# Attention values by feature: values as the loaded operand in two halves of the array, probabilities divided before their transposes

## The chip, the cores and the metric

The kernel runs on one core of a Trainium2 chip. The metric is the device time of one execution in microseconds (us). TensorE (PE in the rows) multiplies, VectorE (DVE), ScalarE (ACT) and GpSimd (POOL) work element by element, and 16 DMA engines bring the weights. Each engine takes its instructions in the order of the built program.

## What is computed

Two layers of a decoder trunk on one sequence of 256 tokens with 1024 features, in float32. A layer has a mixer (8 causal attention heads of 64 features beside 4 groups of pooling channels, joined by one output projection) and a gated MLP with a short convolution. With one block of 256 keys, the attention is plain causal attention:

```
q, k, v, pz = split(h @ w_in)                       # 4 x 512 columns
p  = softmax(mask(q @ k.T * 64**-0.5))              # per head, 256 x 256, causal
ao = p @ v                                          # per head, 256 x 64
merged = concat(rms_norm(ao, attn_out_gain),        # over 512 features
                rms_norm(pool(pz), pool_out_gain))
x = x + gt1 * rms_norm(merged @ w_out, g_post_mix)
```

The heads are taken in pairs; a pair fills a chunk of 128 features, and there are four chunks, 0 to 3, in each layer.

## The kernel before

Weights stream in 1 MB pieces through four buffers on the SP queue (class `Stream`). Each piece is split into a high and a low float32r part by a cast on ACT (`hi`, L104) and a subtraction on DVE (`lo`, L105), and each large product is three TensorE instructions (`mm3`, L130 to L132). DVE also computes adaLN's dot products (L255), which come in among the mixer's steps.

The mixer's steps stand in the strings `ORDER` (L32), one per layer, in order of priority; from them and from its own estimates the tile framework writes each engine's instruction list. The steps around the change:

- `sc` (L545, L554): scores of a chunk, one bank of PSUM a head. DVE adds the mask and takes the row maximum (L560) and scales it (L563); ACT takes the exponential and its row sums (L567). Tokens are on partitions; per head there is a 128x128 piece (first 128 queries) and a 128x256 piece.
- `pt` (L570): three 128x128 transposes a head on TensorE (L576), copied by ACT to `pts` (L578): keys are then on partitions.
- `at` (L580): `pts` is the loaded operand, 128 columns, and 64 columns of `v` stream (L588). Six products a chunk, 12 instructions, since each float32 product is two passes. Tokens are on partitions in `ao`. DVE takes the reciprocal of the row sums (L592) and multiplies it in (L594, to `an`); ACT squares `an` and sums it by row, one instruction for each block of 128 tokens (L599, counted under `mean_sq`, L335).
- `tr` (L601): two transposes of `an` (L604) put features on partitions, and `merge` (L607) makes high and low parts with the gain, ACT (L609) and then DVE (L610).
- `as` (L672): DVE adds the four chunks' sums of squares (L675, L676), POOL takes the powers and a product (L677 to L680): 1 / rms of the attention group, and the ratio to the pool's.
- `gt` (L306): the gate: transposes `gT` (L299), two adds on DVE (L303, L304), a product (L313), then the transposes `gps` (L319). `ps` (L683): DVE scales the identity by POOL's ratio (`dg`, L687), and eight products with it (L693) bring the pool group to features. `wo` (L708) is the output projection `y` by chunk, 12 products each; the tail's last four chunks need `ps`.

Of the kernel before, what the change touches and what calls it, by code (L numbers as in the profile page):

```python
# [19 lines left out]
RAW_BUFS = 4      # weights as they come, 1 MB each  # L20
PART_BUFS = 8     # high and low parts, 128 x 1024 each
LEAD = 6          # parts made ahead of the tensor engine
ACT_BUFS = 13
DEFER = 6         # last chunks of the down projection, done one token block after the other
LAG = 2           # the down projection's distance behind the up projection
W4_BUFS = 7

# The mixer's steps in order of priority, per layer. kq: queries and keys to features; sc: scores and
# softmax; pt: probabilities transposed; at: values weighted; tr: attention to features; as: its sums;
# ph: pool projection; pc: its copy; sr: pool scale as a row; wi: windows; wp: pool products; ps: pool to  # L30
# features; gp, gt: gate; s2: scale of the next norm; wo: output projection; ah: parts of weights ahead.
ORDER = [  # L32
# [4 lines left out]
]  # L37

# columns of the per-feature vectors, per layer
# [5 lines left out]
class Stream:  # L45
    """Weights in the order of use: loads run RAW_BUFS ahead, parts LEAD ahead."""
# [7 lines left out]
    def load(self, dst, src):  # L54
        """A load to a place of its own, in its turn."""
        self.add(src, dst)
        self.done[-1] = True
# [35 lines left out]
    def ahead(self, n=LEAD):  # L93
        """High and low parts of the next weights: w = hi + lo exactly, both float32r."""
# [24 lines left out]
def trunk(ctx: ExitStack, tc: tile.TileContext, x, c, ct, vec, ident_d, tab_d, w_a1, w_gt, w_s2, w_g2,  # L119
# [125 lines left out]
    def table(func):  # L245
        """Brings the activation's table in ahead of its use."""
        tc.keep_in_program_order(nc.scalar.activation(dummy, dummy, func))

# [1 line left out]
    def dots(l, i, chs):  # L250
        """mod = silu(c) . w_ada + b_ada for two chunks of 128 columns."""
        t = st.raw(i)
        for n, ch in enumerate(chs):
            w = t[:, n * D:(n + 1) * D]
            nc.vector.tensor_tensor_reduce(  # L255
                w, w, cbc, 1.0, vecs[:, l, V_BADA + ch:V_BADA + ch + 1], op0=OP.mult, op1=OP.add,
                accum_out=mod[l][:, ch:ch + 1])
        st.free(i)
# [17 lines left out]
    def ada_gt(l, f, u, tag):  # L276
        """One round of a group of 1024 columns on the tensor engine: four column groups, rows alike."""
# [16 lines left out]
    def group_cols(l, f, s0, tag):  # L294
        """The group's columns to features on partitions, with their bias."""
# [10 lines left out]
    def gate_tile(l, f, tag):  # L306
        """gt * g_post as a row, on every partition."""
# [16 lines left out]
    def pre_coef(l, f, j0, j1):  # L324
        """A = (1 + sc) * g_pre for feature chunks j0..j1."""
# [11 lines left out]
    def rstd(ms, name):  # L337
        """(sum of the two mean squares + eps) ** -0.5."""
# [21 lines left out]
    def tail(mms, ys, g, ra, after):  # L360
        """Last products of each half of each block of tokens, and the block's way through the norms."""
# [30 lines left out]
    class Normed:  # L392
        """Chunks of the modulated norm as high and low parts, made from xn as asked for."""
# [13 lines left out]
        def make(self, j, src, on_act, b=None, between=None):  # L407
            """The chunk for both blocks of tokens, or for one."""
# [21 lines left out]
    def mixer(l, xn, gap):  # L430
# [5 lines left out]
        def w_in(o, k, b, w, c0, n=1):  # L436
            """Columns c0.. of the chunk's weights for one block of tokens, 512 to a bank."""
# [7 lines left out]
        if l == 0:  # L445
            # all columns at once, while the first weights come in
# [57 lines left out]
        # rotary on queries and keys while tokens are on partitions, then features  # L504
# [18 lines left out]
        def qk_trans(i, c2):  # L523
            """Chunks 2 c2, 2 c2 + 1 of the queries (i = 0) or the keys."""
# [15 lines left out]
        # causal attention, two heads to a chunk of 128 features  # L540
        rows = ((0, slice(0, 128)), (1, slice(128, 384)))
        sm, stt, pts, scp, outs, merged = {}, {}, {}, {}, {}, {}
        ssq = small(8, "ssq", 1).rearrange("p (b c) -> p b c", b=2)
# [10 lines left out]
        def soft_a(ch):  # L554
            sm[ch] = wk.tile([128, 2, 384], F32, tag="sm", name="sm", bufs=2)
            s_ = stt[ch] = small(16, "st")
            for hd in range(2):
# [7 lines left out]
                for b, sl in rows:  # L565
                    i = hd * 2 + b
                    nc.scalar.activation(sm[ch][:, hd, sl], sm[ch][:, hd, sl], AF.Exp, scale=0.125,  # L567
                                         bias=s_[:, 4 + i:5 + i], accum_out=s_[:, 8 + i:9 + i])

# [10 lines left out]
        def attend(ch):  # L580
            """Values weighted, then over the rows' sums; two heads side by side, tokens on partitions."""
            ao = bank("ps", "ao")
            for b in range(2):
                for hd in range(2):
                    o = ao[:, b * 128 + hd * 64:b * 128 + hd * 64 + 64]
                    for i in range(b + 1):
                        c0 = i * 512 + (2 * ch + hd) * 64
                        nc.tensor.matmul(o, pts[ch][:, hd, (b + i) * 128:(b + i + 1) * 128],  # L588
                                         vt[:, c0:c0 + 64], start=(i == 0), stop=(i == b),
                                         skip_group_check=True)  # L590
            s_ = stt[ch]
            nc.vector.reciprocal(s_[:, 12:16], s_[:, 8:12])  # L592
            an = outs[ch] = wk.tile([128, 256], F32, tag="an", name="an", bufs=2)
            nc.vector.tensor_mul(  # L594
                an.rearrange("p (b h d) -> p b h d", b=2, h=2),
                ao[:, 0:256].rearrange("p (b h d) -> p b h d", b=2, h=2),
                s_[:, 12:16].rearrange("p (h b) -> p b h", b=2)[:, :, :, None].to_broadcast([128, 2, 2, 64]))
            for b in range(2):
                mean_sq(an[:, b * 128:(b + 1) * 128], ssq[:, b, ch:ch + 1], 1.0 / 16.0)  # L599

        def attn_trans(ch):  # L601
            p = bank("ps", "aT")
            for b in range(2):
                nc.tensor.transpose(p[:, b * 128:(b + 1) * 128], outs[ch][:, b * 128:(b + 1) * 128], ident)  # L604
            merge(ch, p[:, 0:256], vecs[:, l, V_AGAIN + ch:V_AGAIN + ch + 1])
# [7 lines left out]
        # pooling channels  # L613
# [17 lines left out]
        def windows():  # L631
            """Windowed means less the token itself, as products with banded matrices over tokens."""
# [15 lines left out]
        def scale_row():  # L648
            """The pool's scale as a row, on every partition."""
# [344 lines left out]
```

## Time and profile before

| | |
|---|---|
| median of 3 runs | 611.97 us (611.96 to 611.98) |
| profiled execution: first to last instruction | 609.5 us |
| own time of the profiled execution | not listed apart; the runs' median is 2.5 us above the span |
| PE busy | 591.2 us, 97% |
| DVE busy | 482.1 us, 79% |
| ACT busy | 365.3 us, 60% |
| POOL busy | 23.8 us, 4% |
| weights and input read | 147.41 MB, 244 GB/s over the span |

The span is the execution's time from its first to its last instruction; around it lie a start and an end that no row shows. Attention takes some 40 us of each layer: from 59 to 101 us in layer 0 and from 354 to 394 us in layer 1. In both layers the output projection's products run on to the end of the mixer, at about 116 and 408 us. The rest is the combined input projection and the MLP, which the change does not touch.

### The profile page before, as it was taken

The numbers are of one execution on the slowest core, as the hardware profiler recorded it, in microseconds if no ns is written. First come the engines' busy times: TensorE is split into PE (matmuls) and PEld (weight loads), VectorE is DVE, ScalarE is ACT, GpSimd is POOL, SyncE is SP. The second block draws the span as 40 slices with busy tenths as digits, with TensorE's granted clock in tenths as the row PEclk, the third lists the DMA queues.
The fourth block names the chain that finished last, engine by engine and source line by source line (L and its number), as shares of the span: only waits on it lengthen the run. The fifth ranks groups of instructions, "written<-read, shape, count | busy, mean of one in ns | idle before, by whom it ended". The sixth has DMA issues, their size and how long they took to land.

```text
span 609.5 us, 9880 instructions
## 1 busy us (share of the span) xinstructions
PE 591.2 (97%) x3836; PEld 516.4 (85%) x3836; DVE 482.1 (79%) x847; ACT 365.3 (60%) x657; POOL 23.8 (4%) x64
## 2 busy tenths in 40 slices
PE   5999899999999999999999999999999999999995
PEld 3887578699999999999858878868999999999984
DVE  5998588679999998978558699555999887777753
ACT  4456787496466565566347578638755655656641
POOL 1000011200000000000010000110000000000001
PEclk9999999999999999999999999999999999999998
DMA  8999787867988877765419857526677766455001
GB/s 304 401 396 358 305 282 272 303 260 279 338 304 312 304 298 294 261 232 183 139 64 363 340 174 275 184 82 274 268 276 276 276 219 253 166 192 206 2 1 69
DMA packets 22769, 149.10 MB, mean 245 GB/s; under 512 B 2881, under 2 KB 3265, under 8 KB 6210
## 3 DMA queue, kind: packets, MB, share of 16 engines
q1 hardware_dynamic: 22722, 148.47, 65.7%
q8 instruction: 30, 0.49, 0.3%
q14 instruction: 17, 0.14, 0.1%
HBM read 147.41 MB, written 1.05 MB: 244 GB/s over the span
## 4 chain that ended last, share of the span: by engine, by line
PE 89%; DVE 5%; DMA 2%; ACT 2%; POOL 1%; issue 1%; POOLq 0%; SPq 0%; DVEq 0%; ACTq 0%
PE u L796 41%; PE d L130 7%; PE d L132 7%; PE d L131 7%; PE qk L131 2%; PE qk L130 2%; PE qk L132 2%; PE y L130 2%; PE y L132 2%; PE y L131 2%; DVE lo L105 1%; DMA raw<-w_up_d 1%; PE pz L130 1%; PE v L130 1%; PE pz L132 1%; PE pz L131 1%
## 5 line engine op out<-in xcount | busy, mean ns | idle before, releaser
L105 DVE TENSOR_TENSOR lo<-raw,hi 128x1024 fp32r<-128x1024 f32 (+1 forms) x184 | 217.7, 1196 | 27.4 <-ACT hi L104 27.2
L104 ACT CAST hi<-raw 128x1024 fp32r<-128x1024 f32 (+1 forms) x184 | 186.0, 1034 | 66.5 <-PE u L796 19.0
L796 PE MATMUL u<-hh,hi 128*128 128x256 f32 x704 | 182.0, 282 | 0.5 <-ACT hh L417 0.5
L796 PE MATMUL u<-hh,lo 128*128 128x256 f32 x704 | 181.8, 281 | 0.0
L796 PE MATMUL u<-hl,hi 128*128 128x256 f32 x704 | 138.5, 282 | 0.0
L796 PEld LDWEIGHTS u<-hh,hi 128*128 128x128 f32 x704 | 132.5, 188 | 2.2 <-ACT hh L417 0.9
L796 PEld LDWEIGHTS u<-hh,lo 128*128 128x128 f32 x704 | 132.5, 188 | 1.4
L796 PEld LDWEIGHTS u<-hl,hi 128*128 128x128 f32 x704 | 107.0, 188 | 0.0
L255 DVE CUSTOM_DVE_ANT_0 raw<-raw,cbc,vecs 128x1024 f32<-128x1024 f32 x64 | 81.1, 1276 | 0.6 <-DMA raw<-w_g_d 0.4
L806 ACT ACTIVATE cv<-u,vecs 128x256 f32<-128x256 f32 x88 | 48.7, 561 | 50.2 <-PE u L796 50.2
L130 PE MATMUL d<-hi,sh 128*128 128x512 f32 x176 | 69.5, 395 | 0.0
L131 PE MATMUL d<-lo,sh 128*128 128x512 f32 x176 | 69.2, 393 | 0.0
L132 PE MATMUL d<-hi,sl 128*128 128x512 f32 x176 | 68.9, 394 | 0.0
L807 DVE SCALAR_TENSOR_TENSOR cv<-u,vecs,cv 128x255 f32<-128x255 f32 x88 | 41.7, 478 | 22.5 <-ACT cv L806 22.1
L809 DVE SCALAR_TENSOR_TENSOR cv<-u,vecs,cv 128x254 f32<-128x254 f32 x88 | 41.6, 478 | 1.6
L132 PEld LDWEIGHTS d<-hi,sl 128*128 128x128 f32 x176 | 33.0, 188 | 7.9 <-DVE sl L816 0.2
L130 PEld LDWEIGHTS d<-hi,sh 128*128 128x128 f32 x176 | 33.1, 188 | 6.5 <-ACT sh L815 0.4
L131 PEld LDWEIGHTS d<-lo,sh 128*128 128x128 f32 x176 | 33.2, 189 | 6.1
L815 ACT CAST sh<-cv 128x256 fp32r<-128x256 f32 x44 | 17.6, 405 | 31.3 <-DVE cv L813 31.3
L812 ACT ACTIVATE cv<-cv 128x256 f32<-128x256 f32 x44 | 18.3, 417 | 15.1 <-DVE cv L809 15.0
L130 PE MATMUL y<-hi,mgh 128*128 128x512 f32 x64 | 26.0, 406 | 0.0
L132 PE MATMUL y<-hi,mgl 128*128 128x512 f32 x64 | 25.5, 399 | 0.0
(144 smaller groups left out, 737.0 us busy)
## 6 DMA issues: line engine op xcount, KB each, us to landing
raw<-w_up_d SPq DMA_DIRECT2D x44, 1024.0 KB, 4.9
raw<-w_down_d SPq DMA_DIRECT2D x22, 1024.0 KB, 4.9
raw<-w_gt_d SPq DMA_DIRECT2D x16, 1024.0 KB, 5.0
raw<-w_a_d SPq DMA_DIRECT2D x15, 1024.0 KB, 6.5
raw<-w_out_d SPq DMA_DIRECT2D x8, 1024.0 KB, 5.6
raw<-w_s_d SPq DMA_DIRECT2D x8, 1024.0 KB, 5.2
raw<-w_g_d SPq DMA_DIRECT2D x8, 1024.0 KB, 4.9
raw<-w_in_d SPq DMA_DIRECT2D x6, 1024.0 KB, 6.8
```

What stands on the lines that cost most here:

```text
L104: nc.scalar.copy(hi[:, :b - a], src)
L105: nc.vector.tensor_sub(lo[:, :b - a], src, hi[:, :b - a].bitcast(F32))
L130: nc.tensor.matmul(o, lh, rh, start=start, stop=False, skip_group_check=True)
L131: nc.tensor.matmul(o, lh, rl, start=False, stop=False, skip_group_check=True)
L132: nc.tensor.matmul(o, ll, rh, start=False, stop=stop, skip_group_check=True)
L255: nc.vector.tensor_tensor_reduce(w, w, cbc, 1.0, vecs[:, l, V_BADA + ch:V_BADA + ch + 1], op0=OP.mult, op1=OP.add, accum_out=mod[l][:, ch: ...
L796: nc.tensor.matmul(o, w[:, cs], r, start=(k == 0 and i == 0 and w is wh and not low), stop=(k == NK - 1 and low), skip_group_check=True)
L806: nc.scalar.activation(t[:, i], p, AF.Identity, scale=cw[2], bias=cb)
L807: nc.vector.scalar_tensor_tensor(t[:, i, 1:], p[:, :S - 1], cw[1], t[:, i, 1:], op0=OP.mult, op1=OP.add)
L809: nc.vector.scalar_tensor_tensor(t[:, i, 2:], p[:, :S - 2], cw[0], t[:, i, 2:], op0=OP.mult, op1=OP.add)
L812: nc.scalar.activation(t[:, 0], t[:, 0], AF.Silu)
L815: nc.scalar.copy(sh, t[:, 0])
```

## The change

`tr` is gone from both strings of `ORDER`; the other steps keep their order. The softmax divides its probabilities on DVE, per head. `at` loads `v` (64 columns a head) and streams `pts`: the first block of keys meets all 256 queries, the second block the last 128. Head 0 writes partitions 0 to 63 and head 1 partitions 64 to 127, each in its own half of the array's columns. The result has features on partitions, so `merge` reads it at once; ACT squares it whole, POOL adds the four chunks' squares element by element, and two products with a column of ones sum over features. Comments are gone from the file, so its line numbers differ.

```diff
@@ soft_a(ch), for each head hd
+                nc.vector.reciprocal(s_[:, 12 + 2 * hd:14 + 2 * hd], s_[:, 8 + 2 * hd:10 + 2 * hd])
+                for b, sl in rows:
+                    i = hd * 2 + b
+                    nc.vector.tensor_scalar(sm[ch][:, hd, sl], sm[ch][:, hd, sl], s_[:, 12 + i:13 + i], None,
+                                            op0=OP.mult)
@@ attend(ch)
-            for b in range(2):
+            for i in range(2):
                 for hd in range(2):
-                    o = ao[:, b * 128 + hd * 64:b * 128 + hd * 64 + 64]
-                    for i in range(b + 1):
-                        c0 = i * 512 + (2 * ch + hd) * 64
-                        nc.tensor.matmul(o, pts[ch][:, hd, (b + i) * 128:(b + i + 1) * 128],
-                                         vt[:, c0:c0 + 64], start=(i == 0), stop=(i == b),
-                                         skip_group_check=True)
-            ...
+                    c0 = i * 512 + (2 * ch + hd) * 64
+                    nc.tensor.matmul(ao[hd * 64:hd * 64 + 64, i * 128:256], vt[:, c0:c0 + 64],
+                                     pts[ch][:, hd, i * 256:i * 128 + 256], start=(i == 0), stop=(i == 1),
+                                     skip_group_check=True, tile_position=(0, 64 * hd))
+            merge(ch, ao[:, 0:256], vecs[:, l, V_AGAIN + ch:V_AGAIN + ch + 1])
+            sq = wk.tile([128, S], F32, tag="an", name="an", bufs=2) if ch else ssq
+            nc.scalar.activation(sq, ao[:, 0:256], AF.Square, scale=1.0 / 16.0)
+            if ch:
+                nc.gpsimd.tensor_tensor(ssq, ssq, sq, op=OP.add)
-        def attn_trans(ch):
-            ...
@@ attn_sums()
-            nc.vector.tensor_reduce(t[:, 0:2], ssq, axis=mybir.AxisListType.X, op=OP.add)
-            nc.vector.tensor_scalar(t[:, 0:2], t[:, 0:2], 0.5, EPS, op0=OP.mult, op1=OP.add)
+            p = bank("ps", "ss")
+            for b in range(2):
+                nc.tensor.matmul(p[:, b:b + 1], ssq[:, b * 128:(b + 1) * 128], ones, start=True, stop=True)
+            nc.vector.tensor_scalar(t[:, 0:2], p[:, 0:2], 0.5, EPS, op0=OP.mult, op1=OP.add)
```

In the instruction lists this shows at three places of layer 1. The first is DVE's list between the maxima of chunk 0's second head and the copy of `pz` (`sm` the probabilities, `st` their sums and reciprocals, `raw` and `mod` adaLN's dot products). Before:

```order
L105 TENSOR_TENSOR lo<-raw,hi 128x1024
L563 TENSOR_SCALAR st<-st 128x2
L255 ISA raw,mod_78<-raw,cbc,vecs 128x1024
L255 ISA mod_78 128x1
L592 RECIPROCAL st<-st 128x4 x2
L329 SCALAR_TENSOR_TENSOR coef_80<-mod_78,vecs 128x2
```

and in the change:

```order
L105 TENSOR_TENSOR lo<-raw,hi 128x1024
L572 TENSOR_SCALAR sm<-sm,st 128x128
L572 TENSOR_SCALAR sm<-sm,st 128x256
L569 RECIPROCAL st<-st 128x2
L563 TENSOR_SCALAR st<-st 128x2
L255 ISA raw,mod_78<-raw,cbc,vecs 128x1024
L255 ISA mod_78 128x1
L572 TENSOR_SCALAR sm<-sm,st 128x128
L572 TENSOR_SCALAR sm<-sm,st 128x256
L569 RECIPROCAL st<-st 128x2
L329 SCALAR_TENSOR_TENSOR coef_80<-mod_78,vecs 128x2
L105 TENSOR_TENSOR lo<-raw,hi 128x1024
```

The pairs of `sm` are, in this order, chunk 1's second head and chunk 0's first; chunk 0's second head follows behind the last row shown. The `st` at L563, which the last exponentials of chunk 0 wait for, has moved behind a pair and a reciprocal.

The second place is TensorE's list for chunk 0, from its transposes `pT` (`qT` are the transposes of queries and keys for chunks 2 and 3). Before:

```order
L576 MATMUL pT<-ident,sm 128x128 x6
L529 MATMUL qT<-ident,qk_3657 128x128
...
L588 MATMUL ao<-v,pts 128x64 x6
L652 MATMUL psr<-ident,vecs 128x128 x4
L576 MATMUL pT<-ident,sm 128x128 x6
L604 MATMUL aT<-ident,an 128x128 x2
```

and in the change:

```order
L581 MATMUL pT<-ident,sm 128x128 x3
L591 MATMUL ao<-pts,v 64x256
L581 MATMUL pT<-ident,sm 128x128 x3
L529 MATMUL qT<-ident,qk_3645 128x128
...
L591 MATMUL ao<-pts,v 64x256
L591 MATMUL ao<-pts,v 64x128 x2
L645 MATMUL psr<-ident,vecs 128x128 x4
L581 MATMUL pT<-ident,sm 128x128 x6
```

The first head's long product now stands between the two heads' transposes, ahead of the eight `qT`.

The third place is DVE's list behind the last attention product of layer 1. Before:

```order
L675 TENSOR_REDUCE ra<-ssq 128x2
L303 TENSOR_TENSOR mod_78<-gT,vecs 128x8
L676 TENSOR_SCALAR ra<-ra 128x2
L304 TENSOR_TENSOR mod_78<-gT,mod_78 128x8
L313 TENSOR_TENSOR coef_80<-mod_78,vecs 128x8
L687 TENSOR_SCALAR dg<-ident,ra 128x128 x2
```

and in the change:

```order
L671 TENSOR_SCALAR ra<-ss 128x2
L682 TENSOR_SCALAR dg<-ident,ra 128x128
L303 TENSOR_TENSOR mod_78<-gT,vecs 128x8
L682 TENSOR_SCALAR dg<-ident,ra 128x128
L304 TENSOR_TENSOR mod_78<-gT,mod_78 128x8
L313 TENSOR_TENSOR coef_80<-mod_78,vecs 128x8
```

The first `dg`, which waits for POOL, now stands ahead of the gate's three instructions. On TensorE the `gps` (which read `coef`) stand ahead of the eight products with `dg`, in both kernels.

## Rows read from the trace of the kernel before

**Rows 1.** The page's first part: busy time, share of the span and instructions of each engine.
```profile
PE 591.2 (97%) x3836; PEld 516.4 (85%) x3836; DVE 482.1 (79%) x847; ACT 365.3 (60%) x657; POOL 23.8 (4%) x64
```

**Rows 2.** Busy time by stage: from and to (us), length, busy time of each engine with its count, granted TensorE clock, DMA share and GB/s. The first is layer 1, the others layer 0.
```profile
356.00:372.00 16.00, 16.00 (x107) 13.33 (x106) 15.94 (x47) 11.60 (x33) 0.00 (x0) 1.00 0.65 236
...
60.00:76.00 16.00, 13.46 (x106) 8.53 (x104) 9.59 (x42) 11.46 (x36) 0.00 (x0) 1.00 0.82 316
76.00:92.00 16.00, 15.29 (x108) 12.55 (x105) 13.58 (x28) 12.96 (x34) 2.42 (x2) 1.00 0.78 273
92.00:104.00 12.00, 11.62 (x73) 9.80 (x72) 10.34 (x29) 8.93 (x22) 2.94 (x4) 1.00 0.75 266
```

**Rows 3.** The chain that ended last, through layer 1's mixer: start, length (us), what.
```profile
366.00 0.65 PE pT L576 x6
...
367.53 1.29 PE ao L588 x12
...
369.91 0.28 PE aT L604 x2
370.18 0.43 PE sc L551 x4
...
372.41 1.48 PE ao L588 x12
373.89 0.29 PE y L130
...
375.35 0.22 PE aT L604 x2
...
387.03 1.28 PE ao L588 x12
...
392.69 1.78 PE pT L693 x16
...
408.18 0.25 PE y L132
```

**Rows 4.** The gate's rounds L283, which use the array in four column groups of 32, 8 instructions a round: how many are under way in three moments of the round at 75.21 us (from and to, length, PE busy with count, PEld busy with count, clock, DMA).
```profile
75.30:75.35 0.05, 0.05 (x4) 0.00 (x0) 1.00 0.06 0
75.65:75.70 0.05, 0.05 (x8) 0.00 (x0) 1.00 0.00 0
75.85:75.90 0.05, 0.05 (x4) 0.00 (x0) 1.00 0.00 0
```

**Rows 5.** The chain around other rounds of L283: what follows one in layer 0, and the four ahead of layer 1's input projection (the next product of the same kind, with nothing ahead of it but its like, is the last row).
```profile
61.91 0.99 PE gacc L283 x8
62.90 0.38 PE qT L529 x2
...
319.68 0.43 PE qk L130
...
320.57 0.23 PE qk L130
```

**Rows 6.** Instructions of two lines on TensorE: count, least/median/greatest duration in ns, first and last start, shapes.
```profile
L283 PE MATMUL gacc<-raw,ctt x128: 592/592/616, 61.8 to 411.4; 128*32 128x512 f32 x128
...
L552 PE MATMUL sc<-k,q x32: 376/377/378, 64.4 to 372.0; 64*128 64x256 f32 x32
```

**Rows 7.** Groups on DVE, POOL and ACT by shape: line, engine, operation, out<-in, count, busy us, mean ns of one, idle time before.
```profile
L687 DVE TENSOR_SCALAR dg<-ident,ra 128x128 f32<-128x128 f32 x4 | 1.0, 284 | 2.7 <-POOL ra L678 2.7
L357 DVE TENSOR_SCALAR xn<-x,rx 128x512 f32<-128x512 f32 x12 | 5.3, 481 | 5.1 <-POOL rx L342 5.1
L592 DVE RECIPROCAL st<-st 128x4 f32<-128x4 f32 x8 | 1.3, 167 | 2.1 <-ACT sm L567 2.1
L594 DVE TENSOR_TENSOR an<-ao,st 128x256 f32<-128x256 f32 x8 | 3.4, 420 | 6.8 <-PE ao L588 6.7
...
L341 POOL TENSOR_TENSOR ry<-ry,msy 128x1 f32<-128x1 f32 x8 | 1.5, 190 | 20.1 <-ACT sqs L335 20.1
L677 POOL TENSOR_TENSOR ra<-ra,powc 128x2 f32<-128x2 f32 x2 | 2.5, 1254 | 9.7 <-DVE mod L304 5.0 <-DVE coef L329 4.7
L679 POOL TENSOR_TENSOR ra<-ra,powc 128x2 f32<-128x2 f32 x2 | 1.4, 688 | 0.0
...
L335 ACT ACTIVATE sqs<-an 128x128 f32<-128x128 f32 x16 | 5.0, 313 | 2.7 <-DVE an L594 2.3 <-DVE coef L329 0.3
L609 ACT ACTIVATE mgh<-aT,vecs 128x256 fp32r<-128x256 f32 x8 | 3.8, 473 | 0.7 <-PE aT L604 0.7
```

**Rows 8.** DVE and ACT in order of time around chunk 0's last exponentials in layer 1: start, length, engine, line, what.
```profile
363.06 0.16 DVE L563 TENSOR_SCALAR st<-st 128x2 f32<-128x2 f32 x1
363.13 1.27 DVE L255 CUSTOM_DVE_ANT_0 raw<-raw,cbc,vecs 128x1024 f32<-128x1024 f32 x1
363.66 0.49 ACT L567 ACTIVATE sm<-sm,st 128x256 f32<-128x256 f32 x1
364.15 1.04 ACT L104 CAST hi<-raw 128x1024 fp32r<-128x1024 f32 x1
```

**Rows 9.** TensorE and DVE in layer 0, in order of time: the last attention product's multiplication and the products of the pool group.
```profile
94.03 0.42 DVE L594 TENSOR_TENSOR an<-ao,st 128x256 f32<-128x256 f32 x1 [0.25 <-PE ao L588]
...
99.28 2.41 PE L693 MATMUL pT<-dg,pz 128*128 128x128 f32 x16 [0.26 <-DVE dg L687]
```

**Rows 10.** Who waited for whom on TensorE from 56 to 124 us: total us, times, longest.
```profile
PE aT L604 <- DVE an L594: 0.6, 1, 0.6
```

More of the change, by code (lines that the diff above doesn't have):

```diff
@@ L541, in mixer @@
         rows = ((0, slice(0, 128)), (1, slice(128, 384)))
-        sm, stt, pts, scp, outs, merged = {}, {}, {}, {}, {}, {}
-        ssq = small(8, "ssq", 1).rearrange("p (b c) -> p b c", b=2)
+        sm, stt, pts, scp, merged = {}, {}, {}, {}, {}
+        ssq = small(S, "ssq", 1)
         def scores(ch):
@@ L582, in attend @@
             ao = bank("ps", "ao")
-            for b in range(2):
+            for i in range(2):
                 for hd in range(2):
-                    o = ao[:, b * 128 + hd * 64:b * 128 + hd * 64 + 64]
-                    for i in range(b + 1):
-                        c0 = i * 512 + (2 * ch + hd) * 64
-                        nc.tensor.matmul(o, pts[ch][:, hd, (b + i) * 128:(b + i + 1) * 128],
-                                         vt[:, c0:c0 + 64], start=(i == 0), stop=(i == b),
-                                         skip_group_check=True)
[L591 to L599, printed above, removed]
-        def attn_trans(ch):
[L602 to L605, printed above, removed]
+                    c0 = i * 512 + (2 * ch + hd) * 64
[7 more added lines that the diff above has]
+                nc.gpsimd.tensor_tensor(ssq, ssq, sq, op=OP.add)
         def merge(k, p, gain):
@@ L744, in step @@
                 attend(i)
-            elif f == "tr":
-                attn_trans(i)
             elif f == "wo":
```

8 rows, old and new, of the table ORDER are left out of this document.

## The prediction, made before the changed kernel was run

> **What bounds the kernel now.** I read the page's totals first: TensorE is busy 591.2 of 609.5 us [rows 1], so its own work is worth something wherever it never waits. The change lies in two stretches of some 40 us, so I read those by stage [rows 2]. In layer 1 TensorE is busy for all of 356 to 372 us, and DVE for 15.94 of 16: TensorE sets the end, and DVE has no room beside it. In layer 0 TensorE is busy 13.46 of 16, 15.29 of 16 and 11.62 of 12 us: it waits at first and little later. The clock is 1.00 in every stage (the upper level, 2.4 GHz) and the work stays as dense, so I take no change of the clock. Last I read the chain through layer 1's mixer [rows 3]: it stays on TensorE from the transposes at 366.00 to the last product of `y` at 408.18, so each instruction removed there brings the end forward and each new wait puts it back.
>
> **TensorE's own work, per layer.** Removed: the four `ao` of 12 instructions, 1.29 + 1.48 + 1.28 and one that I take at 1.29, together 5.34 us, and the four pairs of `aT`, 0.28 and three of 0.22, 0.94 us [rows 3]. Added: a chunk has four products of two passes each. The price of a pass comes from two shapes [rows 6]: 512 columns last 592 ns and 256 columns 377 ns, so 256 more columns cost 215 ns, and 128 cost 108. One head is then 2 x (215 + 108) = 0.65 us. Whether both heads run at once decides much. Nothing here uses two halves of the array, but the gate's rounds use four quarters: four passes are under way at 75.30, eight around the change, four again at 75.85 [rows 4]. So four passes stream together, and I let two do the same: 0.65 us for both heads. A round of 2 x 0.43 takes 0.99, so 0.13 on top; behind it two transposes take 0.38 in place of 0.22 and a product 0.43 in place of 0.23 [rows 5], so 0.2 for the way back to the whole array. That is 0.98 a chunk. In layer 1 the list splits chunk 0: the first head's long product goes alone (0.43 + 0.2), which makes 1.61. The two `ss` are four loads of 128 columns; an `ao` instruction, bound by the same load, takes 1.29 / 12 = 0.107, so 0.43 in all. Layer 1: 3 x 0.98 + 1.61 + 0.43 = 4.98 against 6.28, **1.3 us less**. Layer 0, without a split: 3.92 + 0.43 = 4.35, **1.9 us less**.
>
> The Trainium skill (TensorEngine Tiling (Array Packing), Performance Considerations) advises just this swap where the streamed side has 64 columns or fewer, and its Theoretical Speedup gives up to 2x. An estimate by it would take 2.7 us from each layer's `ao`; the rows give 0.8 and 1.4, since the old form was bound by its loads and the new one pays for entering and leaving the halves. What the full gain would make of the time is the first rival.
>
> **DVE's work.** Added a chunk: two divisions of 128x128, two of 128x256, two reciprocals, less one reciprocal and `an` at 0.42. A division has no row of 128x256; 128x128 takes 0.28 and 128x512 0.48 [rows 7], so 0.35 between them. Neighbours overlap by 0.08 (0.16 long, the next 0.07 later [rows 8]), so a pair holds DVE for 0.5 and a reciprocal for 0.1. Net +0.8 us a chunk, 3.2 a layer. Most of it is covered by postponing dot products, which nothing in the mixer needs soon; where it is not, it shows as the waits below. ACT loses two squares of 0.31 with their reads and gains one of 0.45 (like `mgh`, 0.47 [rows 7]): a little less work, worth nothing by itself.
>
> **New waits in layer 1.** I followed the lists with these durations.
> - Chunk 0. L563 of its second head stood at 363.06 [rows 8]. It now stands behind two pairs, three reciprocals and a wait for ACT's row sums, so near 364.7, and those exponentials end at 365.65, not near 364.1. The first head's division comes behind a dot product (1.27) and ends at 366.45; the second's behind a reciprocal and a `lo`, at 368.3. TensorE is free at 366.00 as before. It waits 0.5 for the first head's rows, then 0.6 for ACT to copy its transposes (the long product is next in the list), then 0.3 for the second head. **+1.4.** Behind it the scores of chunks 2 and 3 took 2.23 us (370.18 to 372.41 [rows 3]) where 16 instructions of 0.107 need 1.72; they now come so late that their operands are there: **-0.5**.
> - `ss`. Behind the last `ao` come `mgh` (0.47), the pool's square that ACT has before the next (0.8 with its read), two squares (0.45 each) and POOL's add. No row shows POOL adding 128x256: below 0.19 it can't be (one element a partition), above it could be 1.25 like a power [rows 7]. I take 0.6: POOL's 0.19 to start and 0.42 for the same shape on DVE, the nearest row in size. The chain is 2.9 us with its hand-overs; TensorE has ten products of `y`, 2.3 us, to fill it. **+0.5.**
> - `gps`. DVE's list has `dg` ahead of the gate's adds. From the end of `ss`: L671 0.15, two powers of 0.69, a product of 0.19, then `dg`, add, `dg`, add, product, 0.8: 2.5 us before `gps` can start, against `gT` (0.44) and five products of `y` (1.16) on TensorE. **+0.9.**
>
> The Trainium skill (GPSIMD Engine Reference, Engine selection) puts two-input elementwise work on GpSimd at about twice VectorE's time. An estimate by it is 0.84 us for the add, and the wait at `ss` 0.25 longer; no run here shows that add yet.
>
> Layer 1: -1.3 - 0.5 + 1.4 + 0.5 + 0.9 = **+1.0 us**.
>
> **Layer 0.** TensorE's work falls by 1.9, and the wait of 0.6 for `an` [rows 10] goes. In its place: chunk 1's first transposes wait 0.9, because ACT now copies chunk 0's first transposes ahead of chunk 1's exponentials and DVE divides only behind them; chunk 2's `ao` waits 0.7 for the copies, which stand behind chunk 3's exponentials and both pool squares on ACT; chunk 3's waits 0.45 for its own copies. At the end, the old kernel has `an` at 94.03, a wait of 0.26 for `dg`, and 2.41 us for products that take 1.78 in layer 1 [rows 3, 9]; the new one waits for `gps` about as long. Layer 0: -1.9 - 0.6 + 2.05 = **-0.5 us**.
>
> No DMA is added or removed, and SP's list keeps its order. Weight buffers come free with `hi`/`lo`, which move by a microsecond or so; the MLP that follows is bound by TensorE and has its pieces in hand.
>
> **Sum.** 609.5 + 1.0 - 0.5 = 610.0 us of span. The runs' median is 2.47 above the span shown, and nothing in the change touches what lies around it: 612.5 us.
>
> **Rivals.**
> 1. *TensorE's saving lands.* The divisions and copies find slack that my walk misses (a dot product elsewhere, an earlier sum), and the waits of layer 1 mostly vanish. For it: layer 1's chain is TensorE alone [rows 3]. Against it: DVE is full there [rows 2]. It gives -1.3 in layer 1 and about -1.3 in layer 0 (half of its new waits): 609.4 us. The Trainium skill's 2x, above, would end here or lower.
> 2. *The sums of squares become the path, and it is slower.* Square, POOL's add, `ss`, POOL's powers, `dg`, `gps` stand in one row at the end of attention in both layers. If POOL's add takes 1.25 and a power too, as the mean of L677 [rows 7], layer 1 loses 0.65 + 0.55 more and layer 0, where that power took longest, 1.0: 614.7 us. It decides from where the chain is longer than the 15 products of `y` and `gT` in its shade. For it: POOL's times scatter from 0.69 to 1.25. Against it: POOL has nothing else to do.
> 3. *The halves do not run together.* Two heads one after the other cost 0.65 more, eight times: 617.7 us. Against it stands [rows 4].
>
> **How the numbers follow.** Within 0.2% (1.22 us, about what a measurement of this kernel can tell) means 610.75 to 613.19. The forecast has 0.48: 0.43 within and 0.05 above, as its waits sum errors of some tenths each. Rival 1 has 0.20, rival 2 0.27, rival 3 0.05. Faster 0.20, same 0.43, slower 0.37. The range, 609.5 to 614.9, leaves out rival 3, about half of rival 1 and the top of rival 2; it covers the add at 0.19 (-0.4) and at 1.25 (+0.65).
>
> **What would show each step.** `ao` as eight instructions of about 0.8 us, and a first product behind it of 0.43; both heads' passes under way at once. In layer 1, TensorE idle ahead of chunk 0's transposes and its first `ao` (1.4 us), ahead of `ss`, and ahead of `gps`, where it had no idle time at all. Divisions near 0.28 and 0.35. Layer 1's last `y` near 408.7 where layer 0 gives back 0.5, and layer 0's end half a microsecond early. The prediction is wrong if layer 1 shows no such waits, or if `ao` takes 1.3 us.

## The result, and the profile after

The changed kernel takes 616.42 us (median of four runs, 615.26 to 618.09) against 611.98: a ratio of 1.0075, 95% interval 1.0063 to 1.0087. It is slower by 4.4 us; the forecast was 612.5 with a range to 614.9, so both missed. Timed again beside the experiments it took 615.66. The span shown is 613.4 us, 3.9 more than before; it is that of the fastest of the four runs.

The totals first, to read against [rows 1]:

```profile
PE 588.5 (96%) x3796; PEld 508.1 (83%) x3796; DVE 488.8 (80%) x877; ACT 363.7 (59%) x633; POOL 29.5 (5%) x70
```

TensorE is busy 2.7 us less and the span is 3.9 longer, so the loss is waiting. Where, the stages tell (columns as in [rows 2]; the last two lines are the end of layer 1's attention, where the old kernel had TensorE busy 4.00 of 4.00 in both):

```profile
60.00:76.00 16.00, 12.56 (x100) 8.29 (x101) 12.96 (x57) 10.67 (x34) 0.00 (x0) 1.00 0.83 326
76.00:92.00 16.00, 15.36 (x105) 10.62 (x97) 12.70 (x28) 13.86 (x31) 1.83 (x3) 1.00 0.71 263
92.00:104.00 12.00, 10.22 (x63) 7.96 (x62) 9.11 (x22) 5.54 (x12) 5.14 (x6) 1.00 0.73 263
...
356.00:372.00 16.00, 15.43 (x90) 11.53 (x89) 15.53 (x48) 11.16 (x27) 0.00 (x0) 1.00 0.60 199
...
389.00:393.00 4.00, 2.77 (x14) 1.98 (x12) 0.48 (x1) 3.89 (x8) 2.32 (x4) 1.00 0.39 166
393.00:397.00 4.00, 2.85 (x21) 2.31 (x21) 1.90 (x7) 1.35 (x3) 1.84 (x4) 1.00 0.00 0
```

Chunk 0's region loses 0.57 us (356 to 372), the eight microseconds behind the last `ao` lose 2.38, and layer 0 loses most at the same place, 92 to 104. The waits on TensorE name the partner (us in total, times, longest), first of layer 1 (350 to 420 us):

```profile
PE ss L670 <- POOL ssq L598: 1.2, 1, 1.2
PE gps L319 <- DVE coef L313: 1.1, 1, 1.1
PE ao L591 <- ACT pts L583: 0.6, 1, 0.6
PE pT L581 <- DVE sm L572: 0.5, 1, 0.5
```

and of layer 0 (56 to 126 us; the wait for `an` of [rows 10] is gone):

```profile
PE sc L551 <- DVE k L531: 2.1, 2, 1.2
PE gps L319 <- DVE coef L313: 1.0, 1, 1.0
PE ss L670 <- POOL ssq L598: 0.8, 1, 0.8
...
PE gT L299 <- ACT grow L291: 0.7, 1, 0.7
PE y L130 <- ACT mgh L602: 0.6, 1, 0.6
PE pw L634 <- DVE st L560: 0.6, 1, 0.6
```

Of the 2.1 at `sc`, 1.6 were there before; the other five are new. The `pw` are the pool's products.

The chain through the end of layer 1's attention (start, length, what) shows what stood behind those two waits:

```profile
388.92 0.13 PE ao L591 x2
...
389.45 0.72 ACT sqs L335 x2
...
390.25 0.20 POOL rp L662
...
390.53 0.23 POOL rp L663
390.76 0.44 issue
391.20 0.74 POOL ssq L598
...
392.01 0.73 POOL ssq L598
...
392.79 0.62 PE ss L670 x4
...
393.43 0.17 DVE ra L671
...
393.67 0.71 POOL ra L672
394.37 0.66 POOL ra L674
395.03 0.17 POOL ra L673
...
395.22 0.28 DVE dg L682
...
395.58 0.19 DVE dg L682
...
395.88 0.18 DVE coef L313
...
396.20 1.06 PE gps L319 x8
```

From the end of the last `ao` at 389.05 to `gps` at 396.20 are 7.15 us, and of these the chain is on TensorE for the 0.62 of `ss` alone. ACT makes the pool's squares first; then GpSimd's list holds the pool's `rp`, its scaling and its power, ahead of the adds, and **both** late adds, chunk 2's and chunk 3's, run one behind the other. In the old kernel [rows 3] the same stretch never left TensorE.

As a measure for what follows: layer 1's mixer, from its first `pz` product to its last `y` product, takes 56.0 us from the start of the one to the start of the other before (352.0 to 408.0) and 58.8 after (353.1 to 411.9). Layer 0's, from its first `qT` to the first up-projection product `u`, takes 62.7 before (60.1 to 122.8) and 63.5 after (60.4 to 123.9). So layer 1 loses 2.8 us and layer 0 loses 0.8; the 0.2 that layer 0 begins late lies in a stretch that the change does not touch.

### The profile page after: what moved, and what is told of

The parts are those of the page before. It is cut to its first block, busy times and chain, and to the rows that moved or that the text cites. A ratio compares the mean times of both kernels' runs of the same rounds, so it can differ in the third digit from the quotient of the medians.

```text
span 613.4 us, 9822 instructions
## 1 busy us (share of the span) xinstructions
PE 588.5 (96%) x3796; PEld 508.1 (83%) x3796; DVE 488.8 (80%) x877; ACT 363.7 (59%) x633; POOL 29.5 (5%) x70
## 4 chain that ended last, share of the span: by engine, by line
PE 85%; DVE 6%; ACT 4%; POOL 2%; issue 2%; DMA 1%; POOLq 0%; SPq 0%; DVEq 0%; ACTq 0%
PE u L789 41%; PE d L130 7%; PE d L132 7%; PE d L131 7%; PE qk L130 3%; PE qk L131 2%; PE qk L132 2%; ACT sqs L335 1%; PE y L132 1%; PE pz L130 1%; PE y L130 1%; DVE raw L255 1%; PE pz L131 1%; PE pz L132 1%; PE v L130 1%
## 5 line engine op out<-in xcount | busy, mean ns | idle before, releaser
L130 PE MATMUL qk<-hi,hh 128*128 128x512 f32 x64 | 23.0, 419 | 2.9 <-ACT hh L417 2.9
```

Of the source, the lines that this page charges most:

```text
L130: nc.tensor.matmul(o, lh, rh, start=start, stop=False, skip_group_check=True)
```

## The experiments

Theory A: the loss is the chain of sums of squares, which now leaves through GpSimd. Theory B: it is the division on VectorE. Theory C: the division is the smaller part that A leaves over. Theory D: the swap saves nothing that counts. All kernels were timed in five rounds beside the kernel before, on three chips in all; its medians there were 611.64 to 611.97 us. Differences between runs below are of medians, and a few tenths of them can be the chip; the ratio is taken to the kernel before on the same chip.

| run | us | ratio to before, 95% | layer 1's mixer, us | layer 0's mixer, us |
|---|---|---|---|---|
| before | 611.97 | | 56.0 | 62.7 |
| after | 616.42 | 1.0075 [1.0063, 1.0087] | 58.8 | 63.5 |
| e_after | 615.66 | 1.0059 [1.0046, 1.0072] | 58.8 | 63.7 |
| e_add_small | 614.02 | 1.0026 [1.0017, 1.0035] | 57.6 | 62.3 |
| e_add_twice | 618.36 | 1.0100 [1.0086, 1.0114] | 59.9 | 64.8 |
| e_pe_sum | 612.79 | 1.0014 [1.0005, 1.0023] | 56.7 | 62.8 |
| e_add_dve | 613.36 | 1.0021 [1.0012, 1.0029] | 56.9 | 62.8 |
| e_nopow | 613.65 | 1.0029 [1.0020, 1.0037] | 57.5 | 62.9 |
| e_dve_nopow | 611.89 | 0.9992 [0.9983, 1.0001] | 55.5 | 62.2 |
| e_before_nopow | 612.23 | 1.0003 [0.9995, 1.0011] | 56.0 | 62.4 |
| e_swap | 611.27 | 0.9986 [0.9978, 0.9995] | 56.1 | 61.7 |
| e_div_only | 614.78 | 1.0056 [1.0036, 1.0075] | 58.1 | 63.2 |
| e_pe_act | 614.22 | 1.0032 [1.0020, 1.0044] | 57.0 | 64.3 |
| e_gt_first | 617.98 | 1.0098 [1.0085, 1.0112] | 58.8 | 65.5 |
| e_pe_ord | 614.40 | 1.0039 [1.0027, 1.0052] | 59.5 | 62.8 |
| e_pe_ordgt | 614.44 | 1.0042 [1.0029, 1.0056] | 57.8 | 63.6 |
| e_dve_gt | 614.61 | 1.0043 [1.0031, 1.0056] | 56.7 | 63.9 |

The two last columns are of one profiled execution each. Their sum follows the times of those executions within about a microsecond; what remains is mostly when layer 0 begins, 60.0 to 61.8 us from one profile to the next, whatever the kernel.

The program's scheduler sorts the work anew for each edit. In `e_add_small`, `e_add_twice` and `e_nopow` TensorE's list stayed the same but for a few products of `y`; in the others more moved.

### The adds: less, more, elsewhere

The anchor. 

> The changed kernel once more, as the anchor for the runs beside it on this chip: 616.4 us, 4.4 above the kernel before (4.0 to 5.2). No theory speaks for another value.

It came to 615.66, 3.9 above the kernel before, just under that range; its waits in layer 1 are those of the changed kernel's first profile to 0.1 us.

`e_add_small`:
```
-  nc.gpsimd.tensor_tensor(ssq, ssq, sq, op=OP.add)
+  nc.gpsimd.tensor_tensor(ssq[:, 0:256:16], ssq[:, 0:256:16], sq[:, 0:256:16], op=OP.add)
```


> Leaves out most of the sums of squares: GpSimd's three adds a layer take 16 of the 256 columns, all other work and nearly all of the order stay. Theory A (the loss sits in the chain of sums of squares: last squares, GpSimd's `rp`, two adds of 0.73 one behind the other, `ss`, the powers, `dg`, `gps`): each add falls to about 0.2, so layer 1 gets back about 1.0 and layer 0 1.0 to 1.8 (one of its adds took 1.59): 613.9 us (613.3 to 614.5), and the wait at `ss` in layer 1 shrinks from 1.2 to 0.2 or less. Theory B (the loss is the division on VectorE, ahead of the transposes of the probabilities): 616.2, since the adds would lie in the shade of something else.

`e_add_twice`:
```
   nc.gpsimd.tensor_tensor(ssq, ssq, sq, op=OP.add)
+  nc.gpsimd.tensor_tensor(sq, sq, ssq, op=OP.mult)
```


> Adds behind each of GpSimd's adds a product of the same 128x256 that nobody reads: the suspected cost is doubled, the order stays. Theory A: the product behind the third chunk's add stands ahead of the last add, so layer 1 loses another 0.73, layer 0 0.75 to 1.6, and the last product delays the powers little: 618.2 us (617.5 to 619.0), wait at `ss` in layer 1 near 1.9. Theory B: 616.4 to 616.7.

`e_pe_sum`:
```
-  if ch:
+  if ch == 1:
       nc.gpsimd.tensor_tensor(ssq, ssq, sq, op=OP.add)
...
-  nc.tensor.matmul(p[:, b:b + 1], ssq[..b..], ones, start=True, stop=True)
+  for ch in (0, 2, 3):
+      nc.tensor.matmul(p[:, b:b + 1], sqs[ch][..b..], ones, start=(ch == 0), stop=(ch == 3))
```


> GpSimd adds chunk 1's squares only (early, nobody waits); chunks 2 and 3 go to TensorE as they are, `ss` has six products of one column where it had two. Theory A: no add is left behind the last square, so layer 1 gets back the wait of 1.2 at `ss` less four more loads of 0.107, and what the earlier powers give at `gps`; layer 0 some 1.0 to 1.8: 613.7 us (613.0 to 614.5). Theory B: 616.4 to 616.8, for the four loads a layer.

All three went A's way, and theory B, by which next to nothing should have moved, falls: 1.6 us less, 2.7 more, 2.9 less than the anchor. Layer 1 follows the add closely: -1.2, +1.1, -2.1. Two details missed. In `e_add_small` 0.5 of the wait at `ss` stays, not 0.2: the two adds take 0.56 together, and `rp` still stands ahead of them. `e_pe_sum` went below A's range, to 612.79. With it the two long waits are gone; what is left of the waits in layer 1's attention is

```profile
PE ao L591 <- ACT pts L583: 0.6, 1, 0.6
PE pT L581 <- DVE sm L572: 0.5, 1, 0.5
```

and the chain of the same stretch stays on TensorE, with `ss` in parts and products of `y` between (start, length, what):

```profile
387.73 0.80 PE ao L591 x8
388.52 0.31 PE ss L672 x2
...
390.77 0.79 PE ss L672 x8
391.56 0.82 PE gps L319 x7
```

The 0.5 at `pT` looks like the division's, but GpSimd has a hand in it. In the changed kernel its early add, chunk 1's, runs beside a dot product until 379.45, and the pair of divisions that these transposes wait for takes 1.01 us where a pair elsewhere takes 0.54 or 0.55 (start, length, engine, line, what):

```profile
377.75 1.70 POOL L598 TENSOR_TENSOR ssq<-ssq,an 128x256 f32<-128x256 f32 x1 [60.88 <-ACT an L596]
...
378.78 1.01 DVE L572 TENSOR_SCALAR sm<-sm,st 128x128 f32<-128x128 f32 x2
```

`e_pe_sum` leaves this add on GpSimd, and the wait stays. In `e_add_small`, where the add is of 16 columns, and in `e_add_dve` below, where it is on VectorE, the same pair takes 0.55 and the wait is gone.

In `e_add_twice`, part of the 2.7 may not be the add: in layer 0, behind a wait of 1.6 us at `ss`, TensorE's granted clock was 0.84, 0.50 and 0.81 in the stages from 98 to 104 us, and products of `y` started 0.43 us apart where they start 0.23 apart otherwise. The wait at `gps` is gone there, so layer 0's 1.1 us cannot be split between the two.

`e_add_dve`: `nc.gpsimd` becomes `nc.vector` in that line. 

> The changed kernel with its three adds a layer on VectorE in place of GpSimd. Theory A: an add of this shape takes 0.42 there, and does not stand behind `rp`, so the two late adds end about 1.2 us earlier in layer 1 and as much in layer 0: 613.5 us (612.9 to 614.3). Rival (VectorE is full, the adds come behind dot products of 1.27 and put the divisions back): 615.5 us (614.8 to 616.5).

613.36, A's number. The add takes 416 ns on VectorE; `ss` no longer waits, `gps` still does (1.2 and 1.4 us).

### The powers behind them

`e_nopow`, `e_dve_nopow` (with `e_add_dve`'s line) and, on the old kernel, `e_before_nopow`:
```
-  nc.gpsimd.tensor_tensor(t[:, 4:6], t[:, 0:2], powc..., op=OP.pow)
+  nc.vector.tensor_tensor(t[:, 4:6], t[:, 0:2], powc..., op=OP.mult)
...   (the lines on t[:, 8:10], t[:, 2:4] and t[:, 6:8] likewise)
```


> Leaves out the two powers between `ss` and `dg`: products of the same two columns on VectorE stand in their place, GpSimd keeps the adds. The order of TensorE's work stays. Theory A: in layer 1 the powers and what follows them on GpSimd take 1.54 us (layer 0: 2.53, its first power standing beside a dot product), small products on VectorE some 0.3: the waits at `gps` (1.2 and 1.0) go, those at `ss` stay: 613.5 us (612.8 to 614.2). Rival (the shade is eaten by the next wait in the row): 615.4 us.

> The same powers left out, and the adds on VectorE: nothing of GpSimd is left between the last `ao` and `dg`. Theory A: the run with its adds on VectorE had 613.4 with waits at `gps` of 1.2 and 1.4; without them 611.3 us (610.6 to 612.2), so the swap with its division stands near the kernel before. Rival (the division alone holds it up by 2 to 3 us): 613.2 us.

> The kernel before with the same powers left out: the control. Theory A: its sums lay in the shade (no wait at `gps`, 0.3 at `pT` for `dg` in layer 0), so 611.6 us (611.2 to 612.0). Rival (the powers cost every version the same): 610 us or less.

`e_nopow` came within 0.2 of its number. Its longest waits in layer 1 are those at `ss`, at chunk 0's `ao` and at `pT`, and `gps` is no longer among them:

```profile
PE ss L670 <- POOL ssq L598: 1.2, 1, 1.2
PE ao L591 <- ACT pts L583: 0.6, 1, 0.6
PE pT L581 <- DVE sm L572: 0.5, 1, 0.5
```

`e_dve_nopow`, with nothing of GpSimd left behind the last `ao`, cannot be told from the kernel before, and the control did not move (612.23 us, interval of the ratio 0.9995 to 1.0011; layer 1's mixer 56.0 in both). So the same powers cost the old kernel nothing that can be measured, and the new one 2.0 us with the late adds on GpSimd (615.66 to 613.65), 1.5 with them on VectorE (613.36 to 611.89); by the ratios it is 1.8 in both. The rival that the next wait takes over is out.

### The division, and the swap by itself

`e_swap` is `e_pe_sum` without the reciprocal and the two `tensor_scalar` products on `sm`. 

> The swap without its division and without the late adds: leaves out the division of the probabilities (reciprocal and both products on VectorE), with the sums of squares as in the run that gives chunks 2 and 3 to TensorE. Theory C (what that run keeps over the kernel before, 1.0 us, is the division on VectorE: 0.5 and 0.6 of waits in layer 1, 0.5 at `sc`, 0.6 at `pw` and 0.6 at `y` in layer 0): 610.8 us (610.0 to 611.6), 1.0 below the kernel before. Theory D (the swap saves TensorE nothing that counts, the division is in the shade): 612.6 us.

`e_div_only` is the kernel before, with those lines put into its softmax, and
```
-  nc.vector.tensor_mul(an..., ao..., reciprocals...)
+  nc.vector.tensor_copy(an, ao[:, 0:256])
```


> The kernel before with the division alone moved: probabilities are divided on VectorE ahead of their transposes, `an` is a plain copy of `ao`, the product and the sums of squares stay as they were. Theory C: the waits for VectorE come without the saving on TensorE: 613.8 us (613.0 to 615.0), 2.0 above the kernel before. Theory D: 611.8 to 612.2.

Theory C holds: `e_swap` is 1.5 us under `e_pe_sum`, and the division put into the old kernel costs it 2.8 us by the medians (ratio 1.0056, interval 1.0036 to 1.0075), more than expected. The two are not the same price: the 1.5 holds the 0.5 at `pT` in which GpSimd's early add has a hand, and `e_div_only` keeps on VectorE a copy of 0.42 us a chunk for `an`, which the changed kernel does not have. `e_div_only` shows the wait for ACT's copies without any swap, beside one for `an`:

```profile
PE ao L593 <- ACT pts L583: 0.6, 1, 0.6
PE aT L604 <- DVE an L597: 0.5, 1, 0.5
```

Theory D is refuted, but what `e_swap` gains is small: 0.7 us of 611.97 (ratio 0.9986, interval 0.9978 to 0.9995). It is no clean price of the swap either: `e_swap` has no division at all, the old one included, and still waits 0.6 for `dg` in layer 1, whose mixer takes 56.1 us, as before. Its gain is in layer 0.

`e_pe_act`: in `e_pe_sum`, the second head's division on ScalarE:
```
+  if hd:
+      nc.scalar.activation(sm[ch][:, hd, sl], sm[ch][:, hd, sl], AF.Copy, scale=s_[:, 12 + i:13 + i])
```


> As the run that gives chunks 2 and 3 of the squares to TensorE, with the division of the second head of each chunk on ScalarE instead of VectorE. Theory C with VectorE as the one that is full: the wait of 0.5 at `pT` and half of layer 0's go: 612.0 us (611.4 to 612.6). Rival (ScalarE's list is as much on the path, since the copies of the transposes stand in it): 613.4 us (612.8 to 614.2).

614.22, the rival's case, at the upper end of its range: the wait at `pT` fell to 0.2, but `ao` now waits 0.7 for `pts` in layer 1 and 1.0 for `psr` in layer 0, both of them copies on ScalarE.

### Filling the shade: four misses

`e_gt_first` moves `gt` ahead of `as` in both layers' lists. 

> The changed kernel with the gate's step ahead of the sums of squares in both lists: `gT` stands right behind the last `ao`, `gps` ahead of `ss`, and VectorE has the gate's adds and product ahead of `dg`. GpSimd's chain keeps its length; TensorE has 1.5 us more to do in its shade. Theory A: from the end of the last `ao` to the second `dg` the chain is 6.7 us in layer 1; `gT`, `gps`, `ss` and thirteen products of `y` are 5.2, so 1.5 us of idle are left of 2.3, and the like in layer 0: 614.3 us (613.7 to 615.0), with no wait at `gps` and one at `pT` for `dg`. Rival (the wait only changes its name): 615.7 us.

617.98, 2.3 us worse than the anchor, and so neither theory's number. The wait at `gps` went as expected; the wait for `dg` took its place, 1.2 us in layer 1, where 1.1 at `ss` stay, and 2.5 in layer 0. Layer 1's mixer is as long as the anchor's, 58.8 us; layer 0's is 1.8 longer. The chain in layer 1 (start, length, what):

```profile
395.60 0.17 DVE ra L671
395.77 0.07 issue
395.84 1.62 POOL ra L672
397.45 0.66 POOL ra L674
```

The power took 1.62 us where it had taken 0.71, and VectorE's list of the same moment (start, length, engine, line, what) shows its neighbour, a `lo` that the new order had let in:

```profile
395.60 0.16 DVE L671 TENSOR_SCALAR ra<-ss 128x2 f32<-128x2 f32 x1 [2.94 <-PE ss L670]
395.68 1.21 DVE L105 TENSOR_TENSOR lo<-raw,hi 128x1024 fp32r<-128x1024 f32 x1
```

The `lo` ends at 396.89, and the power 0.56 later. I had reckoned with 0.7.

`e_pe_ord` is `e_pe_sum` with layer 1's list changed:
```
-  ... ph2 ph3 pt0 kq1 at0 s20 sr pt1 sc2 sc3 at1 wo0 pt3 pc wi pt2 s22 wp
+  ... ph2 ph3 kq1 pt0 sr at0 s20 pt1 sc2 sc3 at1 wo0 pc wi pt3 s22 wp pt2
```


> The run that gives chunks 2 and 3 of the squares to TensorE, with layer 1's list re-arranged for the division: the queries' transposes and the pool scale's row stand ahead of chunk 0's `ao`, the windows ahead of chunk 2's transposes. Layer 0 keeps its list. Theory C (the rest is waits for the division, for want of cover): layer 1's 0.6 at `ao` and 0.5 at `pT` go: 611.7 us (611.1 to 612.3). Rival (VectorE has no room, so the waits turn up at another place): 612.8 us.

614.40. Theory C's wait at `ao` went. The one at `pT` stayed, with GpSimd's early add again beside the divisions (0.77, and 1.02 for the pair), and a new one of 1.2 came at the pool's `pT` for `dg`. Behind it stands the larger loss (from and to, length, busy time of the engines, clock, DMA):

```profile
396.00:398.00 2.00, 2.00 (x12) 2.00 (x11) 1.11 (x3) 1.07 (x3) 0.00 (x0) 0.50 0.00 0
```

After that idle time TensorE was granted 0.50, the lower of its two levels (1.2 GHz), and those `pT` took 3.58 us where `e_pe_sum` needed 1.79. This is the profile of the slowest of the five executions; whether the clock fell in the others no profile shows.

> As the run before it (squares to TensorE, layer 1's list re-arranged), with the gate's step ahead of the sums of squares in both layers too. Theory A: in layer 1 no wait was left there, so nothing; in layer 0, where GpSimd's power took 1.73 us behind six products of `ss`, `gps` no longer has to wait: 611.3 us (610.6 to 612.0), at or under the kernel before. Rival (layer 0 ends with its weights, whatever TensorE does): 611.7 us.

> The changed kernel with its adds on VectorE and the gate's step ahead of the sums of squares. Theory A: the run with the adds on VectorE still waited 1.2 (layer 1) and 1.4 us (layer 0) at `gps`; the gate's work now fills the chain: 612.0 us (611.3 to 612.8). Rival (the waits move to `ss` and `pT`): 613.3 us.

Both add `e_gt_first`'s move, to `e_pe_ord` and to `e_add_dve`. 614.44 and 614.61, misses for either theory: the wait for `dg` in layer 0 is 1.7 and 2.8 us, since GpSimd's first power there took 1.67 and 1.80. So `ss` ahead of the gate, the order of the changed kernel, was the better one twice (`e_after`, `e_add_dve`) and made no difference beside `e_pe_ord`; and no version tried that computes the whole result beats the kernel before; the nearest is `e_pe_sum`. Its sums with chunk 1's add off GpSimd too, which by the rows above would free the divisions, were not run.

## Why the prediction was wrong

**What held.** `ao` is eight instructions of 0.80 to 0.82 us in layer 1 where it is not split (forecast 0.8), the product behind it takes 0.42 to 0.43, and the scores of chunks 2 and 3 take 1.68 where they took 2.23 (forecast -0.5). The halves run together: 0.65 had been worked out for one head, and both take 0.8; the third rival is out. Chunk 0's wait for ACT's copy is 0.6, as forecast. The divisions are 0.35, as forecast, and 0.31 on the mean for 0.28, which holds the one that GpSimd's add held up:

```profile
L572 DVE TENSOR_SCALAR sm<-sm,st 128x256 f32<-128x256 f32 x16 | 5.5, 346 | 0.0
L572 DVE TENSOR_SCALAR sm<-sm,st 128x128 f32<-128x128 f32 x16 | 5.0, 311 | 0.1
```

**The step that failed: the wait at `ss`, +0.5 in layer 1 and nothing in layer 0.** In layer 1 it counted "two squares ... and POOL's add", one add of 0.6, in a chain of 2.9 us. In its place stand `rp` and two adds of 0.74 and 0.73 in one row on GpSimd, and the chain from the last `ao` to `ss` is 3.73 us. The adds belong to chunks 2 and 3, whose `ao` are 1.2 us apart; I asked what GpSimd's add waits for and not what GpSimd's list holds ahead of it. In the old kernel `rp` was over by 385.3 us, and nothing waited behind it. The wait measures 1.2; the add itself was little off, 0.73 for 0.6. The Trainium skill (GPSIMD Engine Reference, Engine selection) has such work at about twice VectorE's time; here it is 0.73 against 0.416, or 1.75 times, measured while VectorE stands idle.

**`gps`, +0.9**, measures 1.1, by the path that I gave: powers, `dg`, the gate's adds, `coef`.

**Chunk 0, +1.4, came to 0.6.** The waits of 0.5 and 0.3 for its divisions are not in the trace. In their place stands the 0.5 at the transposes of 379.59 us, which I had not seen: a pair of divisions there is held up by GpSimd's early add. So 1.1 in all is near the forecast by luck.

**Layer 0, -0.5, failed as a sum.** I had no wait at `ss` in it and took `gps` to wait "about as long" as the old kernel did for `dg`, 0.26. They measure 0.8 and 1.0. The three waits that I did put there, 2.05 together, came at other places: none at chunk 1's transposes or ahead of chunk 2's `ao`; chunk 3's `ao` takes 1.24 in place of 0.80, which is its 0.45; and `sc` +0.5, `pw` 0.6, `y` 0.6 and `gT` 0.7 are waits that I had not named (`e_div_only` has the first three as well). Here the second condition of my second rival was true, GpSimd slow beside VectorE, and it was in my rows: [rows 7] has L677 at a mean of 1.25 us, and I gave it to the rival and not to the forecast. GpSimd and VectorE in layer 0 of the changed kernel (start, length, engine, line, what):

```profile
94.57 2.40 POOL L598 TENSOR_TENSOR ssq<-ssq,an 128x256 f32<-128x256 f32 x2 [4.69 <-ACT an L596]
97.90 1.68 POOL L672 TENSOR_TENSOR ra<-ra,powc 128x2 f32<-128x2 f32 x1 [0.94 <-DVE ra L671]
...
94.65 1.73 DVE L255 CUSTOM_DVE_ANT_0 raw<-raw,cbc,vecs 128x1024 f32<-128x1024 f32 x1
...
97.74 1.28 DVE L255 CUSTOM_DVE_ANT_0 raw<-raw,cbc,vecs 128x1024 f32<-128x1024 f32 x1
```

The two adds take 2.40 (0.75 and 1.59) where layer 1 has 1.53; the dot product that began beside the first takes 1.73, not 1.28. The power ends 0.56 after the dot product beside it. Against this rival I had put that "POOL has nothing else to do", which leaves out what VectorE does to it.

**TensorE's own work, -1.8 in layer 1 with the scores,** shows as -0.7 in busy time (56.40 to 55.72 over the mixer). Counted by rows, `ao` and `ss` come to 3.88 and 0.62, plus some 0.75 for ways back from the halves: 5.25 where I had 4.98, so the saving was near -1.5. The likely rest is the drain at each wait: a product of `y` starts every 0.23 us and ends after 0.39, so about 0.16 of each of the new waits is booked as busy. That split is worked out, not tested.

**The sum.** Layer 1 is 1.8 us worse than forecast, layer 0 1.3, and it begins 0.2 late: 3.3 of the 3.4 between the span's 613.4 and 610.0. The last term, 2.47 from the span to the time, was too large: the later runs of both kernels have 1.7 to 1.9 there, since the span of 609.5 was not that of a median run. The second rival had the right mechanism at the right place, 614.7 us at a chance of 0.27. Its prices were not right: it too counted a single add, and in layer 1 the add took 0.73 and the powers 0.71 and 0.66, not 1.25, so that its number is nearer than the forecast's is in part luck. The experiments give three steps from the anchor to the kernel before: 2.9 for the late adds on GpSimd (`e_after` to `e_pe_sum`), 1.5 for the division (to `e_swap`), and -0.7 for what is left of the change. They are one row of runs, so their sum proves nothing; each step stands on its own run. The powers' 2.0 are not a further term: they are in the same chain, and cost only because the adds and the division have used up its shade.

**Open.** The changed kernel's first four runs spread over 2.8 us (615.26 to 618.09), its five of the second timing over 0.9. The old kernel's, over all of its runs here, go from 611.29 to 613.86. When layer 0 begins accounts for some of that; the clock's fall after a wait, told below, could add to it, but both profiles of the changed kernel show 1.00 in every stage read.

## What to carry to other kernels

When a reduction moves from one engine's instruction into a chain over several, write out each engine's list from the last producer to the first consumer, and count everything in it, including what stood there harmlessly before; then compare the chain with the work in its shade, here 7.15 us against 4.8 for which TensorE had work (the two waits are the rest). A small operation on GpSimd has two prices, alone and beside a large one of VectorE, and a forecast must say which neighbour it will have; an early add that nobody waits for can still hold up a VectorE instruction that somebody waits for. Work that fills a wait can lengthen it, if it lets VectorE in beside GpSimd.

## What the hardware showed unexpectedly

- GpSimd's power on two columns takes 0.68 to 0.71 us beside nothing large, and up to 1.81 where a dot product or a `lo` of VectorE began before it; in every profile it then ends 0.54 to 0.57 us after VectorE's instruction, so it has in effect waited for it. The Trainium skill (GPSIMD Engine Reference, Specifications) says that GpSimd shares its SBUF interfaces with VectorE and contends with VectorE's instructions that run in a 2-port performance mode or have two SBUF inputs; the dot product and `lo` have two, and the traces agree, with a wait of the whole remaining instruction.
- It holds for the division as well, and both ways. Behind a pair of divisions at 88.78 us the changed kernel's power takes 0.89 and ends 0.56 after it; where GpSimd's add is under way first, VectorE is the one held up, 1.73 for a dot product of 1.28 and 1.01 for a pair of divisions of 0.54. A division reads one tensor and a column of factors; whether it runs in such a mode, no run here shows.
- TensorE's granted clock fell to 0.50 behind an idle time of 1.2 us (`e_pe_ord`, above), to 0.50 behind one of 1.6 us (`e_add_twice`) and to 0.56 behind one of 2.5 us (`e_gt_first`, layer 0, 104 to 106 us, where the same `pT` took 3.03 us); it stayed at 1.00 behind 1.2 us in layer 1 of `e_gt_first` and behind the changed kernel's two waits of 1.2 and 1.1. Where it falls, a wait is paid for twice: in `e_pe_ord` 1.2 us of idle time, and 1.8 more for the `pT` behind it.
- Two halves of the array take both heads' products in 0.80 us, where the old form took 1.28 to 1.48 in layer 1: on TensorE the swap did what was hoped of it.
